# Issue order of wide and narrow matmuls in the projections of a two-layer decoder trunk

## The chip, the cores and the metric

The kernel runs on one core of one Trainium2 chip. The metric is the device time of one execution in microseconds (us); lower is better.

## The reference

The kernel computes two decoder layers on 256 tokens of 2048 channels, all in 32-bit floats. Each layer is a mixer and a feed-forward block, and each of the two ends in a residual sum and a layer norm:

```
x <- LN(alpha * x + mixer(x))      # layer 0: state-space scan + block-sparse attention
                                   # layer 1: three-branch sparse attention + retention
x <- LN(alpha * x + ConvFFN(x))
def conv_ffn(x, w_up, conv_w, conv_b, w_down):
    a, u = jnp.split(x @ w_up, 2, axis=-1)          # 2048 -> 2 x 5632
    a = causal_depthwise_conv(a, conv_w, conv_b)
    return (jax.nn.silu(a) * u) @ w_down            # 5632 -> 2048
```

Nearly all the arithmetic is in the projections: `p = h @ w_in` and `@ w_out` of each mixer, and `w_up` and `w_down` of each feed-forward block.

## The kernel before

**Three products for one.** To keep 32-bit accuracy, every operand of a projection is split into a rounded part ("hi") and the exact rest ("lo"). The activations lie in SBUF as `[128, k, hi|lo]`: for each k-tile of 128 input channels, 512 columns, of which the first 256 are the hi parts of the 256 tokens and the last 256 the lo parts. Weights come from HBM in slabs of up to 512 KB (`wraw`, loaded by the queue of SP, line 102); ScalarE makes `whi` from a slab (line 105) and VectorE makes `wlo` (line 106). The kernel needs hi·hi, hi·lo and lo·hi.

**One unit.** The projections that matter here go through `group_b` (line 200): output channels on partitions, 256 of them in a job, which is a *unit* of two halves `o` of 128 channels. Each half has a PSUM accumulator of 512 columns in a bank of its own. For one k-tile and one half there are two matmuls, each with its own load of a 128x128 weight tile:

- a **wide** one, line 236 (line 240 in the last k-tile): `whi` against all 512 columns of the activation, which gives hi·hi in the left 256 columns of the accumulator and hi·lo in the right ones;
- a **narrow** one, line 237 (line 239 in the last k-tile): `wlo` against the first 256 columns, added to the left 256 columns of the same accumulator.

So a k-tile of a unit is four matmuls. Before, the loop over `o` issues both matmuls of half 0 and then both of half 1: wide, narrow, wide, narrow. In the last k-tile the narrow one comes first in each half: narrow, wide, narrow, wide. After it the evacuation `evac` reads both accumulators. The next job uses the other of two accumulator buffers.

**Jobs.** `x` names the activations of an input or "up" projection (16 k-tiles), `y` those of a mixer's output projection (16 k-tiles), `g` those of a "down" projection (44 k-tiles). `group_b` has, by the tables of jobs in the code, 88 jobs of the two up projections, 14 of the down projections, 14 of the mixers' output projections and 34 of the mixers' input projections: (88 + 14 + 34) x 16 + 14 x 44 = 2,792 k-tiles of four matmuls. The first three jobs of each up projection run as one group, with a third unit in the pool `ps`.

**What else runs on TensorE.** `group_one` (lines 191 to 193) handles the last 256 channels of each output and down projection with narrow matmuls alone; `group_a` (lines 266 to 268) puts tokens on partitions; for the values and gates of retention in layer 1 it has wide matmuls alone. In the mixers' input projections and in the first output jobs, small matmuls of attention and scan (`self.fill`) are handed out between k-tiles, for a single unit after every second one.

TensorE runs its matmuls in the order of the program. Nothing in the kernel sets that order but the order in which the Python code issues them.

Of the kernel before, what the change touches and what calls it, by code (L numbers as in the profile page):

```python
# [13 lines left out]
PSUM = bass.MemoryType.PSUM  # L14
# [11 lines left out]
BIG = 1e30  # L26
# [10 lines left out]


def jobs():
    """The weight groups in the order in which they are used: (source, kind, column parts, k-tiles)."""  # L40
    out = []
    dt, v = EV_DT, EV_V
    out += [("ev_in", "A", cols((dt, 16), (v, 336)), KT), ("ev_in", "A", cols((v + 336, 344)), KT),
            ("ev_in", "A", cols((v + 680, 344)), KT)]
    for c in (EV_B, EV_C, *(EV_XS + 256 * i for i in range(4)), *(EV_Z + 256 * i for i in range(4))):
        out.append(("ev_in", "B", cols((c, 256)), KT))
    for i in range(4):
        out += [("ev_in", "B", cols((EV_Q + 256 * i, 256)), KT), ("ev_in", "B", cols((EV_K + 256 * i, 256)), KT)]
    out += out_jobs("ev_out", KT)
    out += ffn_jobs(0)  # L50
    out += [("od_in", "D", cols((OD_RV, 1024)), KT)]
    out += [("od_in", "A", cols((OD_RG + 512 * i, 512)), KT) for i in range(2)]
    out += [("od_in", "A", cols((OD_VS, 256), (OD_G, 24)), KT), ("od_in", "A", cols((OD_VW, 256)), KT)]
    out += [("od_in", "B", cols((c, 256)), KT) for c in (OD_KC, OD_VC, OD_KS)]
    out += [("cmp0", "C", cols((0, 256)), 16), ("od_in", "B", cols((OD_KW, 256)), KT), ("cmp1", "C", cols((0, 256)), 16)]
    out += [("od_in", "B", cols((OD_Q + 256 * i, 256)), KT) for i in range(4)]
    for i in range(4):
        out += [("od_in", "B", cols((OD_RQ + 256 * i, 256)), KT), ("od_in", "B", cols((OD_RK + 256 * i, 256)), KT)]
    out += out_jobs("od_out", KT)
    out += ffn_jobs(1)  # L60
    return out
# [17 lines left out]


class Weights:
    """Streams the weight slabs: load, then a rounded part and the exact rest for the tensor engine."""

    def __init__(self, tc, pool, streams):
        self.tc, self.nc, self.pool, self.slabs, self.done = tc, tc.nc, pool, [], 0
# [34 lines left out]


class Fill:
    """Work of the mixers that is handed out between weight slabs."""

    def __init__(self):
        self.q = []
        self.rate, self.due = 1.0, 0.0

    def add(self, *steps):
        """Steps; a number stands for so many turns without one."""  # L130
        for x in steps:
            self.q += [lambda: None] * x if isinstance(x, int) else [x]

# [23 lines left out]
class Trunk:  # L157
# [12 lines left out]
        self.nc.scalar.activation(hi, src, AF.Copy)  # L170
        self.nc.vector.tensor_tensor(lo, src, hi.bitcast(F32), op=OP.subtract)  # L171

# [1 line left out]
    def apply_to(self, k):  # L174
        while self.applies and self.applies[0][0] < k:
            self.applies.pop(0)[1]()

    def group_one(self, act, evac):
        """128 output channels, all three products summed in one region."""
        nc, w = self.nc, self.w  # L180
        s = w.first[self.job]
        self.job += 1
        nk = act.shape[1]
        acc = self.acc_pool.tile([128, 2, 512], F32, name="acc")[:, 0, :256]
        k = 0
        while k < nk:
            hi, lo = w.get(s)
            s += 1
            for kk in range(hi.shape[1]):
                xh, xl = act[:, k, :256], act[:, k, 256:]  # L190
                nc.tensor.matmul(acc, hi[:, kk, :], xh, start=(k == 0), stop=False)  # L191
                nc.tensor.matmul(acc, hi[:, kk, :], xl, start=False, stop=False)  # L192
                nc.tensor.matmul(acc, lo[:, kk, :], xh, start=False, stop=(k == nk - 1))  # L193
                k += 1
                if k == nk:
                    evac(acc)
                if k % 2 == 0:
                    self.fill.pop()

    def group_b(self, act, evacs, drain=None):  # L200
        """Output channels on partitions, 256 for each of evacs (or 128); act: [128, k, hi|lo]."""
        nc, w = self.nc, self.w
        first = w.first[self.job]
        self.job += 1
        nk = act.shape[1]
        width = w.slabs[first][4]
        accs = [self.acc_pool.tile([128, 2, 512], F32, name="acc") for _ in evacs[:2]]
        units = [[a[:, o, :] for o in range(min(width // 128, 2))] for a in accs]
        if len(evacs) == 3:
            units.append([self.ps(), self.ps()])  # L210
            accs.append(units[2])
        every = 2 if len(evacs) == 1 else 1
        s = first
        k0 = 0
        held = []
        while k0 < nk:
            m = w.slabs[s][3]
            if s == (None if drain is None else first + drain):
                self.fill.flush()
            self.apply_to(k0 + m + 2)  # L220
            hi, lo = w.get(s)
            s += 1
            if len(units) == 3 and k0 == nk - 2:
                held = [(k0, hi[:, 0], lo[:, 0])]
                k0 += m
                continue
            for kk in range(m):
                part = held + [(k0 + kk, hi[:, kk], lo[:, kk])]
                held = []
                c = 0  # L230
                for unit, evac, whole in zip(units, evacs, accs):
                    for k, h, l in part:
                        for o, acc in enumerate(unit):
                            wh, wl = (a[:, c + 128 * o:c + 128 * o + 128] for a in (h, l))
                            if k < nk - 1:
                                nc.tensor.matmul(acc, wh, act[:, k, :], start=(k == 0), stop=False)  # L236
                                nc.tensor.matmul(acc[:, :256], wl, act[:, k, :256], start=False, stop=False)  # L237
                            else:
                                nc.tensor.matmul(acc[:, :256], wl, act[:, k, :256], start=False, stop=False)  # L239
                                nc.tensor.matmul(acc, wh, act[:, k, :], start=False, stop=True)  # L240
                    if k == nk - 1:
                        evac(whole)
                    c += 128 * len(unit)
                if kk % every == every - 1:
                    self.fill.pop()
            k0 += m

    def group_a(self, act, *evacs):
        """Tokens on partitions; up to 512 output channels for each of evacs."""
        nc, w = self.nc, self.w  # L250
        first = w.first[self.job]
        self.job += 1
# [3 lines left out]
        for s in range(KT // m):  # L256
            self.apply_to(m * s + m + 2)
            hi, lo = w.get(first + s)
            for kk in range(m):
                k = m * s + kk  # L260
                for i, (acc, evac) in enumerate(zip(accs, evacs)):
                    wh, wl = (a[:, kk, i * width:(i + 1) * width] for a in (hi, lo))
                    for t in range(2):
                        xh, xl = act[:, k, t * 128:(t + 1) * 128], act[:, k, 256 + t * 128:256 + (t + 1) * 128]
                        o = acc[:, t, :width]
# [18 lines left out]
            else:  # L284
                nc.vector.scalar_tensor_tensor(d, a[:, :, :256], sign, t, op0=OP.mult, op1=OP.add)

# [1 line left out]
    def out_proj(self, act, pool, idx, room):  # L288
        nc, r, w = self.nc, self.r, self.w
        sacc, qacc = room  # L290
# [119 lines left out]
        if not last:  # L410
            self.w.pump(self.w.limit + 1, pin=True)

# [1 line left out]
    def load_consts(self):  # L414
        nc, I, C = self.nc, self.I, self.consts

# [36 lines left out]
        nc.vector.memset(self.mhalf, -0.5)  # L453

    def bias_scratch(self):
        """Row h: -sqrt(128) * bias of distance j - 127, or BIG where the key is later than the query."""
        nc = self.nc
        self.scr = self.dram.tile([8, 384], F32, name="scr")
        with self.tc.tile_pool(name="bias0", bufs=1) as P:
# [8 lines left out]
            nc.sync.dma_start(self.scr, vv)  # L468

    def load_bias(self, pool, tmp_pool):  # L470
        """nb[q, h, c]: the scratch row at distance 128 + q - c."""
        nc = self.nc
        self.nb = pool.tile([128, H, 256], F32, name="nb")
        s = self.scr[:, :]
# [4 lines left out]
            nc.vector.tensor_copy(self.nb[:, 2 * a:2 * a + 2, :], t[:, :, ::-1])  # L479

    def softmax(self, P, S, nb0, nb1, w0, w1, z, stat, j):
        """exp of scores less their maximum; S: negated raw scores (PSUM), z: out, stat[:, j..j+1]: sums."""
        nc = self.nc
        mn = P.tile([128, 2], F32, name="mn", bufs=4)
        for i, (c, n, nb) in enumerate(((0, w0, nb0), (w0, w1, nb1))):
# [8 lines left out]
            self.fill.add(n, a, b)  # L494

    def attn_steps(self, P, y, ct, h, branches, gate=None, cmp=None):
        """Steps of one head. branches: (qT, kT, v columns of tile t); y[:, ct]: result, hi|lo."""
        nc = self.nc
        st = {}
        nbr = len(branches)  # L500
# [71 lines left out]

        return scores, normalise, mix

# [1 line left out]
    def even(self):  # L576
        nc, x = self.nc, self.x
        with ExitStack() as ctx:
# [209 lines left out]
        steps += [diag(7), 4, rms(1), 1, scale(1)]  # L788
        return steps

# [1 line left out]
    def odd(self):  # L792
        nc, x = self.nc, self.x
        with ExitStack() as ctx:
# [99 lines left out]
                self.out_proj(y, P2, 2, (kv["ks"], kv["kw"]))  # L894

    def compress(self, P, i, xh, xl, kcmp, vcmp):
        """Rows of the 34: 16 blocks of 16 tokens for each kv head, then the position rows; columns: first | second half."""
        nc, w = self.nc, self.w
        first = w.first[self.job]
        self.job += 1  # L900
# [94 lines left out]

        return inner, values, turn

# [1 line left out]
    def ffn(self, layer):  # L999
        nc, x = self.nc, self.x  # L1000
        with ExitStack() as ctx:
# [55 lines left out]
        self.ffn(1)  # L1057


# [1 line left out]
def _pack(w, mine):  # L1061
    parts = []
    for kind, spec, nk in mine:
# [78 lines left out]
```

## Time and profile before

| | |
|---|---|
| time, median of 3 runs | 2367.11 us (2366.61 to 2367.96) |
| span of the profiled execution, first to last instruction | 2365.8 us |
| TensorE busy with matmuls | 2332.8 us, 99% of the span, 13,598 matmuls |
| VectorE busy | 1463.9 us, 62% |
| ScalarE busy | 1166.5 us, 49% |
| mean granted clock of TensorE | 0.992 |
| DMA | 426.28 MB, mean 180 GB/s |

The profile gives the profiled execution's own time as its span; the median of the runs lies 1.3 us above it. A matmul's end is modelled and matmuls overlap in the pipeline, so the length in a matmul's row (0.40 us for a wide one) is longer than its share of the time; what counts here is the distance from one matmul's start to the next one's.

### The profile page before, as it was taken

How to read it: one execution, taken by the hardware profiler on the slowest of the kernel's cores; microseconds unless marked ns; L12 is line 12 of the kernel's file. 1: busy time of each engine (PE TensorE's matmuls, PEld its weight loads, DVE VectorE, ACT ScalarE, POOL GpSimd, SP SyncE). 2: the span in 40 equal slices, each digit the busy share in tenths (PEclk: the TensorE clock that was granted, in tenths of full speed). 3: DMA queues.
4: the chain of work that ended last, by engine and by line, in shares of the span. 5: the costliest groups of instructions: out<-in, count | busy, mean ns of one | idle time of the engine just before them, and what ended most of it. 6: DMA issues, size and time to landing. Idle time of an engine off the chain costs nothing.

```text
span 2365.8 us, 34384 instructions
## 1 busy us (share of the span) xinstructions
PE 2332.8 (99%) x13598; PEld 2044.4 (86%) x13598; DVE 1463.9 (62%) x2095; ACT 1166.5 (49%) x1556; POOL 20.4 (1%) x29
## 2 busy tenths in 40 slices
PE   8999999999999999999999999999999999999997
PEld 8888888888888888889789888888888888888887
DVE  5677567766666664555645667768666666654555
ACT  5555545655555554444545553447555555544443
POOL 0001000000000000000000000000000000000000
PEclk9999999999999999999999999999999999999998
DMA  8664554655555555555557634555555555555553
GB/s 252 189 183 150 162 171 146 199 187 187 187 187 186 188 187 187 187 187 180 184 165 227 191 110 145 169 172 170 187 186 185 187 188 187 187 187 187 189 188 114
DMA packets 124673, 426.28 MB, mean 180 GB/s; under 512 B 13872, under 2 KB 18400, under 8 KB 124384
## 3 DMA queue, kind: packets, MB, share of 16 engines
q1 hardware_dynamic: 124512, 424.09, 56.8%
q8 instruction: 106, 1.74, 0.3%
q14 instruction: 55, 0.45, 0.1%
HBM read 421.93 MB, written 2.11 MB: 179 GB/s over the span
## 4 chain that ended last, share of the span: by engine, by line
PE 88%; issue 10%; DVE 1%; DMA 0%; POOL 0%; ACT 0%; ACTq 0%; SPq 0%; POOLq 0%
PE acc L236 47%; PE acc L237 24%; PE acc L240 3%; PE acc L266 2%; PE acc L267 2%; PE acc L268 2%; PE acc L239 1%; PE acc L191 1%; PE acc L192 1%; PE acc L193 1%; PE ps L570 1%; PE ps L236 1%; DVE r L387 0%; PE ps L237 0%; PE ps L509 0%
## 5 line engine op out<-in xcount | busy, mean ns | idle before, releaser
L106 DVE TENSOR_TENSOR wlo<-wraw,whi 128x1024 fp32r<-128x1024 f32 (+5 forms) x818 | 973.0, 1191 | 669.1 <-ACT whi L105 664.1
L236 PE MATMUL acc<-x,whi 128*128 128x512 f32 x3600 | 1291.2, 401 | 3.4 <-DVE x L403 3.4
L105 ACT ACTIVATE whi<-wraw 128x1024 fp32r<-128x1024 f32 (+5 forms) x818 | 844.3, 1033 | 819.9 <-PE acc L236 587.0
L237 PE MATMUL acc<-x,wlo 128*128 128x256 f32 x3600 | 1012.1, 281 | 0.0
L236 PEld LDWEIGHTS acc<-x,whi 128*128 128x128 f32 x3600 | 677.9, 188 | 163.8 <-DVE x L403 4.0
L237 PEld LDWEIGHTS acc<-x,wlo 128*128 128x128 f32 x3600 | 681.8, 189 | 4.7
L236 PE MATMUL acc<-g,whi 128*128 128x512 f32 x1204 | 422.5, 395 | 0.0
L237 PE MATMUL acc<-g,wlo 128*128 128x256 f32 x1204 | 337.7, 280 | 0.0
L236 PEld LDWEIGHTS acc<-g,whi 128*128 128x128 f32 x1204 | 225.8, 188 | 52.9
L237 PEld LDWEIGHTS acc<-g,wlo 128*128 128x128 f32 x1204 | 227.5, 189 | 0.6
L280 ACT ACTIVATE tmp<-acc 128x512 f32<-128x512 f32 x120 | 71.7, 598 | 207.1 <-PE acc L240 207.1
L236 PE MATMUL acc<-y,whi 128*128 128x512 f32 x420 | 150.4, 400 | 0.0
L237 PE MATMUL acc<-y,wlo 128*128 128x256 f32 x420 | 118.1, 282 | 0.0
L266 PE MATMUL acc<-whi,x 128*128 128x512 f32 (+4 forms) x288 | 101.7, 353 | 7.0 <-ACT whi L105 5.9
L267 PE MATMUL acc<-wlo,x 128*128 128x512 f32 (+4 forms) x288 | 101.2, 352 | 0.3 <-DVE wlo L106 0.3
L268 PE MATMUL acc<-whi,x 128*128 128x512 f32 (+4 forms) x288 | 100.7, 350 | 0.0
L236 PEld LDWEIGHTS acc<-y,whi 128*128 128x128 f32 x420 | 79.0, 188 | 17.8 <-DVE y L171 0.3
L240 PE MATMUL acc<-x,whi 128*128 128x512 f32 x240 | 89.9, 396 | 0.0
L237 PEld LDWEIGHTS acc<-y,wlo 128*128 128x128 f32 x420 | 79.4, 189 | 0.8
L1020 DVE SCALAR_TENSOR_TENSOR c<-fpad,prm,c 128x256 f32<-128x256 f32 x176 | 74.1, 480 | 0.1
L239 PE MATMUL acc<-x,wlo 128*128 128x256 f32 x240 | 68.0, 283 | 0.0
L266 PEld LDWEIGHTS acc<-whi,x 128*128 128x128 f32 x288 | 55.8, 194 | 13.4 <-ACT whi L105 5.9
(304 smaller groups left out, 1754.3 us busy)
## 6 DMA issues: line engine op xcount, KB each, us to landing
wraw<-in_up SPq DMA_DIRECT2D x328, 512.0 KB, 4.1
wraw<-in_down SPq DMA_DIRECT2D x174, 512.0 KB, 4.4
wraw<-in_od_in SPq DMA_DIRECT2D x96, 512.0 KB, 3.7
wraw<-in_ev_in SPq DMA_DIRECT2D x72, 512.0 KB, 3.7
wraw<-in_ev_out SPq DMA_DIRECT2D x32, 512.0 KB, 3.5
wraw<-in_od_out SPq DMA_DIRECT2D x32, 512.0 KB, 3.8
wraw<-in_up SPq DMA_DIRECT2D x32, 384.0 KB, 3.1
wraw<-in_ev_in SPq DMA_DIRECT2D x16, 344.0 KB, 3.5
```

The costliest lines, as they stand in the source:

```text
L105: a = nc.scalar.activation(hi[:, :n], raw[:, :n], AF.Copy)
L106: b = nc.vector.tensor_tensor(lo[:, :n], raw[:, :n], hi[:, :n].bitcast(F32), op=OP.subtract)
L191: nc.tensor.matmul(acc, hi[:, kk, :], xh, start=(k == 0), stop=False)
L236: nc.tensor.matmul(acc, wh, act[:, k, :], start=(k == 0), stop=False)
L237: nc.tensor.matmul(acc[:, :256], wl, act[:, k, :256], start=False, stop=False)
L239: nc.tensor.matmul(acc[:, :256], wl, act[:, k, :256], start=False, stop=False)
L240: nc.tensor.matmul(acc, wh, act[:, k, :], start=False, stop=True)
L266: nc.tensor.matmul(o, xh, wh, start=(k == 0), stop=False)
L267: nc.tensor.matmul(o, xh, wl, start=False, stop=False)
L268: nc.tensor.matmul(o, xl, wh, start=False, stop=(k == KT - 1))
L280: nc.scalar.activation(t, a[:, :, 256:], AF.Copy, scale=sign)
L1020: nc.vector.scalar_tensor_tensor(c[:, i, :], pad[:, i, t:t + 256], w[:, t:t + 1], c[:, i, :], op0=OP.mult, op1=OP.add)
```

## The change

In `group_b`, each k-tile of a unit first issues the wide matmuls of both halves and then the narrow ones of both. In the last k-tile both narrow ones come first and then both wide ones. The operands, the accumulators, the number of matmuls and the number of weight loads are the same; the flags `start` and `stop` mark the same wide matmuls as before. The other lines of the diff take out comments and docstrings, so that line numbers shift by up to two.

```
-                        for o, acc in enumerate(unit):
-                            wh, wl = (a[:, c + 128 * o:c + 128 * o + 128] for a in (h, l))
-                            if k < nk - 1:
-                                nc.tensor.matmul(acc, wh, act[:, k, :], start=(k == 0), stop=False)
-                                nc.tensor.matmul(acc[:, :256], wl, act[:, k, :256], start=False, stop=False)
-                            else:
-                                nc.tensor.matmul(acc[:, :256], wl, act[:, k, :256], start=False, stop=False)
-                                nc.tensor.matmul(acc, wh, act[:, k, :], start=False, stop=True)
+                        wide = [(acc, h[:, c + 128 * o:c + 128 * o + 128], act[:, k, :]) for o, acc in enumerate(unit)]
+                        half = [(acc[:, :256], l[:, c + 128 * o:c + 128 * o + 128], act[:, k, :256])
+                                for o, acc in enumerate(unit)]
+                        for i, (acc, wt, mv) in enumerate(wide + half if k < nk - 1 else half + wide):
+                            nc.tensor.matmul(acc, wt, mv, start=(k == 0 and i < len(unit)),
+                                             stop=(k == nk - 1 and i >= len(unit)))
```

On TensorE, at the end of one job of an up projection and the start of the next, the program before has these rows (line, operation, tiles, partitions x columns); the four rows in the middle are the last k-tile of the job, and the next job begins behind them:

```order
L236 MATMUL acc<-x,whi 128x512
L237 MATMUL acc<-x,wlo 128x256
L239 MATMUL acc<-x,wlo 128x256
L240 MATMUL acc<-x,whi 128x512
L239 MATMUL acc<-x,wlo 128x256
L240 MATMUL acc<-x,whi 128x512
L236 MATMUL acc<-x,whi 128x512
L237 MATMUL acc<-x,wlo 128x256
L236 MATMUL acc<-x,whi 128x512
L237 MATMUL acc<-x,wlo 128x256
```

At the same place of the changed program all these matmuls stand at line 237, and like rows are folded (x2, x4):

```order
L237 MATMUL acc<-x,whi 128x512 x2
L237 MATMUL acc<-x,wlo 128x256 x4
L237 MATMUL acc<-x,whi 128x512 x4
L237 MATMUL acc<-x,wlo 128x256 x2
L237 MATMUL acc<-x,whi 128x512 x2
```

What moved: within a job, wide and narrow now come in twos; at the end of a job four narrow ones stand together, and the two wide ones behind them join the next job's first two.

The second place is inside an input job of layer 0's attention, where the two score matmuls of a head (lines 508 and 509) stand between two k-tiles. Before:

```order
L236 MATMUL acc<-x,whi 128x512
L237 MATMUL acc<-x,wlo 128x256
L236 MATMUL acc<-x,whi 128x512
L237 MATMUL acc<-x,wlo 128x256
L508 MATMUL ps<-k,q 128x128
L509 MATMUL ps<-k,q 128x256
L236 MATMUL acc<-x,whi 128x512
L237 MATMUL acc<-x,wlo 128x256
```

In the changed program these two stand at lines 506 and 507:

```order
L237 MATMUL acc<-x,whi 128x512 x2
L237 MATMUL acc<-x,wlo 128x256 x2
L237 MATMUL acc<-x,whi 128x512 x2
L237 MATMUL acc<-x,wlo 128x256 x2
L506 MATMUL ps<-k,q 128x128
L507 MATMUL ps<-k,q 128x256
L237 MATMUL acc<-x,whi 128x512 x2
```

What moved: only the four matmuls of each k-tile among themselves; the small ones stand between the same k-tiles as before. The order of the DMAs and of GpSimd is unchanged; on ScalarE and VectorE a few instructions change places with a neighbour, in the scan of layer 0 and at the start of each up projection.

## Rows read from the trace of the kernel before

**Rows 1.** The page: the span, and part 1, busy time of each engine.

```profile
span 2365.8 us, 34384 instructions
PE 2332.8 (99%) x13598; PEld 2044.4 (86%) x13598; DVE 1463.9 (62%) x2095; ACT 1166.5 (49%) x1556; POOL 20.4 (1%) x29
```

**Rows 2.** The page, part 4: the chain that ended last, by engine.

```profile
PE 88%; issue 10%; DVE 1%; DMA 0%; POOL 0%; ACT 0%; ACTq 0%; SPq 0%; POOLq 0%
```

**Rows 3.** The page, part 5: wide and narrow matmuls on `x`; last, idle time before them.

```profile
L236 PE MATMUL acc<-x,whi 128*128 128x512 f32 x3600 | 1291.2, 401 | 3.4 <-DVE x L403 3.4
...
L237 PE MATMUL acc<-x,wlo 128*128 128x256 f32 x3600 | 1012.1, 281 | 0.0
```

**Rows 4.** Windows inside an up and a down projection: length, busy PE PEld DVE ACT POOL, clock, DMA.

```profile
480.00:880.00 400.00, 400.00 (x2267) 347.37 (x2266) 245.87 (x285) 207.73 (x249) 0.00 (x0) 1.00 0.58 186
910.00:1090.00 180.00, 180.00 (x1030) 157.37 (x1030) 92.16 (x86) 72.32 (x71) 0.00 (x0) 1.00 0.59 188
```

**Rows 5.** The two longest waits of TensorE: who for whom, us in total, times, longest.

```profile
PE acc L266 <- ACT whi L105: 5.9, 1, 5.9
PE ps L359 <- POOL lnst L368: 5.5, 4, 1.6
```

**Rows 6.** Timeline of TensorE inside an up job: start us, us, engine, line, operation.

```profile
702.16 0.40 PE L236 MATMUL acc<-x,whi 128*128 128x512 f32 x1
...
705.34 0.40 PE L236 MATMUL acc<-x,whi 128*128 128x512 f32 x1
```

**Rows 7.** The same inside a down job.

```profile
935.63 0.39 PE L236 MATMUL acc<-g,whi 128*128 128x512 f32 x1
...
942.56 0.39 PE L236 MATMUL acc<-g,whi 128*128 128x512 f32 x1
```

**Rows 8.** The same in `group_a`, wide matmuls alone.

```profile
1173.44 0.39 PE L266 MATMUL acc<-whi,x 128*128 128x512 f32 x1
...
1177.52 0.39 PE L266 MATMUL acc<-whi,x 128*128 128x512 f32 x1
```

**Rows 9.** The same in `group_one`, narrow matmuls alone.

```profile
1119.98 0.28 PE L191 MATMUL acc<-g,whi 128*128 128x256 f32 x1
...
1123.22 0.28 PE L191 MATMUL acc<-g,whi 128*128 128x256 f32 x1
```

**Rows 10.** Timeline where one up job follows another; PEld is the weight load.

```profile
705.93 0.28 PE L237 MATMUL acc<-x,wlo 128*128 128x256 f32 x1
705.93 0.19 PEld L239 LDWEIGHTS acc<-x,wlo 128*128 128x128 f32 x1
706.05 0.28 PE L239 MATMUL acc<-x,wlo 128*128 128x256 f32 x1
706.05 0.19 PEld L240 LDWEIGHTS acc<-x,whi 128*128 128x128 f32 x1
706.17 0.40 PE L240 MATMUL acc<-x,whi 128*128 128x512 f32 x1
...
706.53 0.39 PE L240 MATMUL acc<-x,whi 128*128 128x512 f32 x1
...
706.76 0.39 PE L236 MATMUL acc<-x,whi 128*128 128x512 f32 x1
...
706.98 0.28 PE L237 MATMUL acc<-x,wlo 128*128 128x256 f32 x1
```

**Rows 11.** Timeline: the first wide matmul of the tenth up job after that.

```profile
819.76 0.39 PE L236 MATMUL acc<-x,whi 128*128 128x512 f32 x1
```

**Rows 12.** Timeline: the first wide matmuls of three down jobs that follow each other.

```profile
918.64 0.39 PE L236 MATMUL acc<-g,whi 128*128 128x512 f32 x1
...
949.16 0.39 PE L236 MATMUL acc<-g,whi 128*128 128x512 f32 x1
...
980.24 0.39 PE L236 MATMUL acc<-g,whi 128*128 128x512 f32 x1
```

**Rows 13.** Timeline: three output jobs, first start, and what follows the third.

```profile
336.19 0.39 PE L236 MATMUL acc<-y,whi 128*128 128x512 f32 x1
...
370.09 0.27 PE L191 MATMUL acc<-y,whi 128*128 128x256 f32 x1
```

## The prediction

> **What bounds the kernel now.** I read the page's busy times first: TensorE has work in flight for 99% of the span, VectorE for 62%, ScalarE for 49% [rows 1]. The chain that ended last is 88% TensorE and 10% "issue", that is, time in which nothing visible was waited for [rows 2]. The groups by line say the same from the other side: before the 3,600 wide matmuls on `x` the engine sat idle for 3.4 us in all, before the narrow ones for none [rows 3]. The windows show that this holds in the stretches that matter: for 400 us of an up projection and 180 us of a down projection TensorE is never without work at full granted clock, VectorE is busy for 61% and 51%, ScalarE for 52% and 40%, the DMA engines for 58% and 59% [rows 4]. TensorE's longest waits are 5.9 and 5.5 us [rows 5]. So the time is the sum of the distances between matmul starts, and nothing else can gain or lose much.
>
> I therefore read those distances. In what follows a **pair** is one wide and one narrow matmul.
>
> - Inside an up job nine pairs take 705.34 - 702.16 = 3.18 us [rows 6], 353.3 ns a pair.
> - Inside one of the down jobs twenty pairs take 942.56 - 935.63 = 6.93 us [rows 7], 346.5 ns a pair.
> - Where all are wide, 18 matmuls take 4.08 us [rows 8], 226.7 ns each. Where all are narrow, 27 take 3.24 us [rows 9], 120.0 ns each. Their sum is 346.7 ns.
>
> So the pair costs what its parts cost alone in the down job, and 6.7 ns more in the up job. The difference of wide and narrow, 226.7 - 120.0 = 106.7 ns for 256 columns, is 2.4 columns a ns, the full clock; each matmul has 13.3 ns on top of its columns. What the change can touch is the extra 6.7 ns alone.
>
> **Where the extra sits.** A job is a fixed row of matmuls, so its length can be counted out. Ten up jobs take 819.76 - 706.76 = 113.00 us [rows 10, 11], 11.300 us each. At 346.7 ns a pair the 32 pairs of a job would be 11.093 us; 0.207 us are extra. Call a narrow matmul right behind a wide one a **switch**. The 15 k-tiles wide, narrow, wide, narrow hold 30 of them, the last one (narrow, wide, narrow, wide) holds 1, and 0.207 us over 31 is 6.7 ns. At the end of the job two narrow ones stand together, 0.12 us apart, and the next narrow-to-wide distance is 0.12 us too; two wide ones stand 0.23 us apart and the next distance is 0.22 us [rows 10]. These are the lone values again, to the 0.01 us of the rows. So the extra goes with switches and not with pairs of the same kind.
>
> The down jobs show that the extra isn't always there. One takes 949.16 - 918.64 = 30.52 us, the next 980.24 - 949.16 = 31.08 us [rows 12], against 88 x 346.7 ns = 30.51 us. The first pays 0.01 us, the second 0.57 us, that is 6.6 ns for each of its 87 switches. The same row of matmuls thus runs in one of two rhythms, which a whole job keeps. These two are the second and the third of a layer's seven down jobs; I take it that the rhythms take turns, which makes four long and three short ones in each layer. The ten up jobs are all long, and I take all 88 to be.
>
> **The change, step by step.**
>
> *What all extras sum to now.* Up: 88 jobs x 0.207 = 18.2 us. Down: eight long jobs x 0.57 and six x 0.01 = 4.6 us. Output projections: three jobs take 370.09 - 336.19 = 33.90 us [rows 13], 11.30 each as above, so 14 x 0.207 = 2.9 us. Input projections: 34 jobs, broken by small matmuls; between 0 (the short rhythm) and 0.207 each (the long one), so 0 to 7.0 us; I take the middle, 3.5, since both rhythms have been seen. Together 29.2 us, 27 to 33 us at the bounds.
>
> *What is left after.* Wide, wide, narrow, narrow has one switch where there were two. A 16-tile job has 15 in place of 31 (the last k-tile, narrow, narrow, wide, wide, has none), a 44-tile job 43 in place of 87. If a switch costs what it does now, job by job, 29.2 x 0.49 = 14.2 us are left and **15 us are saved**. If the six short down jobs fall into the long rhythm, they lose 6 x 43 x 6.7 ns = 1.7 us; with the input projections at their bounds the saving is 12 to 17 us.
>
> *What the new order does to waits.* `wlo` of a slab is first needed one wide matmul later, 0.23 us of slack for VectorE; `whi` is needed by the same first matmul as before. In the last k-tile both narrow ones come first, in the fourth part of a slab that has long been ready. The evacuation still waits for the last wide matmul. TensorE waits for none of these in the trace [rows 3, 5], so I cost them at nothing; the cover is the weight slabs' lead. If TensorE runs 1% faster, VectorE, ScalarE and DMA, all near 60% or below [rows 4], have to run 1% faster too, and can.
>
> *ScalarE and VectorE.* A few neighbours change places at the start of each up projection, where TensorE waits for VectorE's layer norm: the whole of that idle time is 3.4 us [rows 3] and GpSimd's part in the norm 5.5 us [rows 5]. I take nothing, with 1 us either way as the bound, a fraction of those.
>
> *The sum.* The span is 2365.8 us, and the median of the runs 1.3 us above it. 2367.1 - 15 = **2352 us**, with 2349 to 2356 as this case's own range.
>
> [...]
>
> **The rivals.**
>
> 1. *No switch costs anything in the new order (28%).* The extra belongs to a rhythm and not to a switch: the short down job has all 87 switches and pays for none [rows 12]. A new row of matmuls may settle in the short rhythm everywhere, since every second distance is now one between equals, and those cost nothing extra [rows 10]. Against it: the same distances stand at each end of an up job, and the job behind falls back to the long rhythm each time. All 29 us would go: 2338 us.
>
> 2. *Nothing changes (14%).* The extra could be the price of a weight load under a narrow matmul. A load begins when the matmul before it starts (at 705.93 and at 706.05) [rows 10], so the load behind a narrow one has 120 ns, and one behind a wide one 227. The new order shuffles which matmul's load that is, but two in four remain: 32 in a job, as before, and 32 x 6.7 ns = 0.213 us fits the 0.207 nearly as well. Against it: the narrow matmuls in a row [rows 9] load under a narrow one each time and have the same 13.3 ns on top as the wide ones [rows 8]. It gives 2367 us. [...]
>
> 3. *Slower: the price is for a change of accumulator bank (11%).* Before, wide and narrow of a half follow each other in one bank, and the bank changes every second matmul, 32 times in a job. After, it changes with every matmul, 64 times. If that is what costs 6.7 ns, a long job pays 0.427 us in place of 0.213; the extras double, and the time is 2367 + 29 = 2396 us. For it: 32 changes fit an up job to 0.007 us. Against it: ten jobs would show 113.07 us, and the rows say 113.00; and in the wide matmuls in a row the bank changes after every third, at the lone 226.7 ns. It decides from the first k-tile on.
>
> The forecast itself, one price for each switch that is left, has 47%.
>
> **How the numbers follow.** Less than 0.2% (4.7 us) is about what a measurement of this kernel can't tell from no change. The forecast and rival 1 are faster: 75%. Rival 2 is the same: 14%. Rival 3 is slower: 11%. For the range I take the forecast, rival 1 with a microsecond on its far side, and most of rival 2, where part of the saving may show: 2337 to 2366 us leaves out rival 3 and the upper half of rival 2, under 2 in 10.
>
> **What would show it.** In the profile after, an up job should last 11.093 + 15 x 0.0067 = 11.19 us; 11.09 is rival 1, 11.30 rival 2, 11.5 rival 3. Inside a job four matmuls should take 700 ns; their four distances should read about 0.23, 0.23, 0.12, 0.12 with 7 ns more in one of them. TensorE's idle time should stay at a few microseconds, and its clock at 0.99. The prediction is wrong if the two new neighbours bring a rhythm of their own with a third price, which no row here can exclude, since the only doublets seen are at the ends of jobs.

## The result and the profile after

The changed kernel takes **2350.69 us** (median of 4 runs, 2349.53 to 2351.00) against 2367.29 us before: 16.6 us less, a ratio of 0.9927 with a 95% interval of 0.9913 to 0.9941. The forecast was 2352 us.

The page after, its span and part 1, answers to [rows 1]:

```profile
span 2348.5 us, 34385 instructions
PE 2315.6 (99%) x13598; PEld 2036.2 (87%) x13598; DVE 1459.7 (62%) x2095; ACT 1161.3 (49%) x1556; POOL 20.8 (1%) x29
```

The span is 17.3 us shorter and the matmuls' busy time 17.2 us. TensorE's two longest waits after are those of [rows 5], under new line numbers:

```profile
PE acc L264 <- ACT whi L105: 5.9, 1, 5.9
PE ps L357 <- POOL lnst L366: 5.5, 4, 1.6
```

The windows after, in the same two projections as [rows 4] (length, busy PE PEld DVE ACT POOL, clock, DMA), still show TensorE without a gap at full granted clock; in 400 us of the up projection it now starts 2,295 matmuls in place of 2,267:

```profile
480.00:880.00 400.00, 400.00 (x2295) 349.65 (x2294) 247.86 (x287) 207.37 (x251) 0.00 (x0) 1.00 0.56 189
910.00:1080.00 170.00, 170.00 (x977) 148.58 (x976) 88.19 (x84) 68.46 (x67) 0.00 (x0) 1.00 0.56 188
```

So the gain is in the distances. In the changed kernel like matmuls at one line are folded into one row, and where two jobs meet, four wide ones stand in one row (x4). Two of those rows ten up jobs apart, two of down jobs that follow each other, and two k-tiles of a down job with 20 k-tiles from the first start to the last:

```profile
600.77 1.09 PE L237 MATMUL acc<-x,whi 128*128 128x512 f32 x4
...
712.44 1.09 PE L237 MATMUL acc<-x,whi 128*128 128x512 f32 x4
...
910.61 1.09 PE L237 MATMUL acc<-g,whi 128*128 128x512 f32 x4
...
941.28 1.09 PE L237 MATMUL acc<-g,whi 128*128 128x512 f32 x4
...
920.14 0.63 PE L237 MATMUL acc<-g,whi 128*128 128x512 f32 x2
920.61 0.39 PE L237 MATMUL acc<-g,wlo 128*128 128x256 f32 x2
...
934.08 0.63 PE L237 MATMUL acc<-g,whi 128*128 128x512 f32 x2
```

An up job lasts 111.67 / 10 = 11.167 us, where it lasted 11.300 [rows 10, 11]. A down job lasts 30.67 us each time; before, 30.52 and 31.08 took turns [rows 12]. Inside a job four matmuls take 13.94 us / 20 = 697 ns, 3.3 ns over the 693.3 of their parts alone; before it was 706.7 in the long rhythm.

Where the 17.3 us come from, by the job starts in the two traces: the jobs of `group_b` got shorter by 11.0 us in the up projections, 2.3 us in the down projections, 1.1 us in the output projections and 2.2 us in the input projections; 0.6 us lie elsewhere. The short jobs of the down projections got 0.15 us longer each.

### The profile page after: what moved, and what is told of

It is laid out like the page before. It is cut to its first block, busy times and chain, and to the rows that moved or that the text cites. A ratio compares the mean times of both kernels' runs of the same rounds, so it can differ in the third digit from the quotient of the medians.

```text
span 2348.5 us, 34385 instructions
## 1 busy us (share of the span) xinstructions
PE 2315.6 (99%) x13598; PEld 2036.2 (87%) x13598; DVE 1459.7 (62%) x2095; ACT 1161.3 (49%) x1556; POOL 20.8 (1%) x29
## 4 chain that ended last, share of the span: by engine, by line
PE 88%; issue 10%; DVE 1%; POOL 0%; DMA 0%; ACT 0%; ACTq 0%; SPq 0%; POOLq 0%
PE acc L237 74%; PE acc L264 2%; PE acc L265 2%; PE acc L266 2%; PE ps L237 1%; PE acc L191 1%; PE acc L192 1%; PE acc L193 1%; PE ps L568 1%; DVE r L385 0%; PE ps L507 0%; PE ps L534 0%; PE ps L506 0%; PE ps L739 0%; DMA wraw<-in_ev_in 0%
## 5 line engine op out<-in xcount | busy, mean ns | idle before, releaser
L237 PE MATMUL acc<-x,whi 128*128 128x512 f32 x3840 | 1201.5, 398 | 3.4 <-DVE x L401 3.4
L237 PEld LDWEIGHTS acc<-x,wlo 128*128 128x128 f32 x3840 | 706.4, 188 | 159.3 <-issue 0.2
L237 PE MATMUL acc<-x,wlo 128*128 128x256 f32 x3840 | 740.4, 279 | 0.0
L237 PEld LDWEIGHTS acc<-x,whi 128*128 128x128 f32 x3840 | 595.4, 189 | 16.5 <-DVE x L401 4.0
L237 PE MATMUL acc<-g,whi 128*128 128x512 f32 x1232 | 385.1, 395 | 0.0
L237 PE MATMUL acc<-g,wlo 128*128 128x256 f32 x1232 | 240.3, 278 | 0.0
L237 PEld LDWEIGHTS acc<-g,whi 128*128 128x128 f32 x1232 | 188.7, 189 | 1.2
L237 PE MATMUL acc<-y,wlo 128*128 128x256 f32 x448 | 86.5, 279 | 0.0
L281 DVE TENSOR_TENSOR u<-acc,tmp 128x512 f32<-128x512 f32 x44 | 30.4, 692 | 53.6 <-ACT tmp L278 53.6
L281 DVE TENSOR_TENSOR fpad<-acc,tmp 128x512 f32<-128x512 f32 x42 | 29.0, 691 | 51.6 <-ACT tmp L278 51.6
```

The costliest lines, as they stand in the source:

```text
L237: nc.tensor.matmul(acc, wt, mv, start=(k == 0 and i < len(unit)), stop=(k == nk - 1 and i >= len(unit)))
L281: nc.vector.tensor_tensor(d, a[:, :, :256], t, op=OP.add)
```

## The experiments

In all of them the extra of a job is its length less 11.093 us (16 k-tiles) or 30.507 us (44 k-tiles), the time of its parts alone. The code shows the lines that carry each change; the flags `start` and `stop` that follow from it are left out where they add nothing.

**1. Turn every second k-tile round.** Theory: a price for each switch (a narrow matmul right behind a wide one). Rivals: a price for a change of accumulator bank, or for a weight load under a narrow matmul.

```
- ... in enumerate(wide + half if k < nk - 1 else half + wide):
+ ... in enumerate(wide + half if k % 2 == 0 else half + wide):
```

> Every second k-tile is turned round: wide, wide, narrow, narrow, then narrow, narrow, wide, wide. A 16-tile job then has 8 narrow-behind-wide switches in place of 15, a 44-tile job 22 in place of 43; loads and changes of accumulator bank are as many as in the changed kernel. If each switch has a price (3.3 ns as inside the changed kernel's jobs, or 6.7 ns as before): an up job of 11.12 to 11.15 us in place of 11.167, and 2343 to 2347 us in all. If the price is for a change of bank, or for a load under a narrow matmul: as the changed kernel, 2351 us.

It took 2360.74 us, ratio 0.9974 (0.9964 to 0.9984): slower than the changed kernel by 10 us, with half its switches. All three theories miss it. The rows of four wide matmuls, ten up jobs apart:

```profile
600.20 1.09 PE L237 MATMUL acc<-x,whi 128*128 128x512 f32 x4
...
712.47 1.09 PE L237 MATMUL acc<-x,whi 128*128 128x512 f32 x4
```

An up job lasts 11.227 us. The extra is 134 ns for 8 switches, 16.7 ns each, where the changed kernel pays 74 ns for 15.

**2. A whole slab of wide, then a whole slab of narrow matmuls.** `wide` and `half` here hold the eight matmuls of a slab of four k-tiles; the group of three jobs at the start of each up projection keeps the order of the changed kernel.

```
...
+ for group in (wide, half) if k0 + m < nk else (half, wide):
+     for acc, wt, mv, k in group:
+         nc.tensor.matmul(acc, wt, mv, start=(k == 0 and group is wide), stop=(k == nk - 1 and group is wide))
```

> For a whole slab of four k-tiles all eight wide matmuls, then all eight narrow ones (in the last slab narrow first). A 16-tile job has 3 switches, a 44-tile job 10. If each switch has a price of 3.3 to 6.7 ns: an up job of 11.10 to 11.11 us, nearly nothing extra left, and 2341 to 2342 us. If the price is for a change of bank or for a load under a narrow matmul: 2351 us. If long runs of narrow matmuls fall behind on their weight loads (eight loads with 120 ns each): slower than the changed kernel, with narrow matmuls more than 120 ns apart.

It took 2350.71 us, ratio 0.9929 (0.9916 to 0.9941), the same as the changed kernel, with a fifth to a quarter of its switches (3 of 15, 10 of 43). Rows of eight narrow, eight wide and the next narrow ones in a down job:

```profile
926.24 1.11 PE L235 MATMUL acc<-g,wlo 128*128 128x256 f32 x8
927.19 2.00 PE L235 MATMUL acc<-g,whi 128*128 128x512 f32 x8
929.03 0.64 PE L235 MATMUL acc<-g,wlo 128*128 128x256 f32 x4
```

Eight narrow ones take 0.95 us, 0.01 less than alone, and eight wide ones 1.84 us, 0.03 more than alone. The distances of those starts in ns, worked out from the trace:

```
narrow  113 119 120 120 120 120 120 120
wide    234 236 228 232 231 227 227 226
```

The narrow ones don't fall behind. It is the first five wide ones after them that are late, 28 ns in all; 8 of these come back in the first two narrow ones. One switch costs 20 ns here. With the price of a switch at 0 or 6.7 (alternation), 3.3 (twos), 16.7 (fours) and 20 ns (eights), **the theory of a fixed price has fallen**.

**3. The same widths, half the changes of bank**: wide 0, wide 1, narrow 1, narrow 0.

```
+ half = half[::-1]
```

> The changed kernel with the two narrow matmuls of a k-tile in the other order: wide 0, wide 1, narrow 1, narrow 0. The row of widths and the switches are the same, but the accumulator bank changes only 2 times a k-tile in place of 4. If the price is for switches: as the changed kernel, 11.167 us an up job and 2351 us. If it is for changes of bank: half of the 11 us that are still extra go, 2345 us.

It took 2350.82 us, ratio 0.9929 (0.9916 to 0.9943), and ten up jobs last the same 111.67 us:

```profile
600.11 1.09 PE L238 MATMUL acc<-x,whi 128*128 128x512 f32 x4
...
711.78 1.09 PE L238 MATMUL acc<-x,whi 128*128 128x512 f32 x4
```

With half the changes of bank the extra is the same; the third rival is out.

**4. Only the last k-tile changed.**

```
+ row = [p for pair in zip(wide, half) for p in pair] if k < nk - 1 else half + wide
```

> Only the last k-tile of a job is changed (narrow, narrow, wide, wide); all others are wide, narrow, wide, narrow as before. A 16-tile job has 30 switches in place of 31. If each switch has a price of 6.7 ns: 11.293 us an up job and 2366.5 us, no difference that can be measured. If the rhythm that a job falls into at its start sets the price, and the end of the job before sets the rhythm: up jobs may become short, 11.09 us, and the time anywhere down to 2340 us.

It took 2360.23 us, ratio 0.9970 (0.9959 to 0.9980). Three wide matmuls now stand together where two jobs meet; four of those rows:

```profile
592.89 0.87 PE L238 MATMUL acc<-x,whi 128*128 128x512 f32 x3
...
603.99 0.85 PE L238 MATMUL acc<-x,whi 128*128 128x512 f32 x3
...
615.29 0.86 PE L238 MATMUL acc<-x,whi 128*128 128x512 f32 x3
...
626.57 0.87 PE L238 MATMUL acc<-x,whi 128*128 128x512 f32 x3
```

The jobs last 11.10, 11.30 and 11.28 us, and this goes on in threes through both up projections: one job in three is short. All 16 k-tiles hold the same matmuls in the same order in each of them, and still the lengths differ; the buffers take turns in twos and fours, the lengths in threes. So what a job takes must depend on the state in which the row before it left TensorE; call that state its **phase**. My new theory was this: **a row of matmuls has rhythms; which one it takes is a matter of phase, and it keeps it until equal neighbours shift the phase.**

**5. No equal neighbours at all.**

```
+ row = [p for pair in zip(wide, half) for p in pair]     # in the last k-tile too
+ ... stop=(k == nk - 1 and mv.shape[-1] == 256)
```

> Wide, narrow, wide, narrow in every k-tile, the last one too, so that a projection is one unbroken alternation over all its jobs; 32 switches a job. Theory of rhythms (an alternating row runs long, 6.7 ns a switch, or short, 0; it keeps its rhythm until two equal neighbours shift its phase): all jobs of an up projection have one length, all 11.307 us (2368 us in all) or all 11.093 us (about 2345 us), with no turns of short and long as in the run with the last k-tile alone changed. Rival, that something at the start of a job (its evacuation, its first weight slab) sets the rhythm: jobs of both lengths again.

The ten runs took 2345.68, 2346.04, 2346.05, 2348.44, 2358.18, 2359.57, 2360.82, 2372.54, 2373.05 and 2377.37 us: one program, 32 us apart, all at a granted clock of 0.992 or 0.993; the ratio of the medians is 0.996 (0.9929 to 0.9992), and says little. The profiled execution is one of the longer ones (2372.54 us, span 2370.5 us); two wide matmuls 320 pairs apart:

```profile
600.19 0.40 PE L238 MATMUL acc<-x,whi 128*128 128x512 f32 x1
...
713.25 0.40 PE L238 MATMUL acc<-x,whi 128*128 128x512 f32 x1
```

That is 113.06 us, 353.3 ns a pair: all its up jobs are long, and both of its down projections too. No turns of short and long are left, as the theory of rhythms expects. The same execution has the short rhythm as well. Three output jobs of layer 0, and the same three of layer 1:

```profile
326.35 0.40 PE L238 MATMUL acc<-y,whi 128*128 128x512 f32 x1
...
360.27 0.40 PE L238 MATMUL acc<-y,whi 128*128 128x512 f32 x1
...
1541.42 0.40 PE L238 MATMUL acc<-y,whi 128*128 128x512 f32 x1
...
1574.70 0.40 PE L238 MATMUL acc<-y,whi 128*128 128x512 f32 x1
```

They take 33.92 us, 11.307 each, and 33.28 us, 11.093 each, with the same matmuls in the same order. So within one execution the unbroken jobs of a projection keep one rhythm or the other. The scatter of the times would then come from what each projection takes at its start: one up projection of 44 jobs, long or short, is 44 x 0.213 = 9.4 us. That the rhythms differ from one execution to the next is argued from the times; only this execution was profiled.

**6. Narrow matmuls of 192 columns**, in the order of experiment 2; the product of the weights' rest is left out for 64 tokens.

```
- half = [(acc[:, :256], ..., act[:, k0 + kk, :256], k0 + kk)
+ half = [(acc[:, :192], ..., act[:, k0 + kk, :192], k0 + kk)
```

> The slab order with narrow matmuls of 192 columns in place of 256: the product of the weights' rest is left out for the last 64 tokens. If columns set the distance of narrow matmuls: 80.0 + 13.3 = 93 ns apart, 27 ns less for each of 5,584, and 2351 - 149 = 2202 us. If the weight load under them sets it: still 113 to 120 ns apart, and about 2351 us, at least 2310.

It took 2310.52 us (one run). Eight wide, eight narrow, and the next wide ones:

```profile
941.84 2.01 PE L235 MATMUL acc<-g,whi 128*128 128x512 f32 x8
943.69 1.03 PE L235 MATMUL acc<-g,wlo 128*128 128x192 f32 x8
944.56 1.78 PE L235 MATMUL acc<-g,whi 128*128 128x512 f32 x7
```

Eight narrow ones take 0.87 us, the first 0.086 (its load lay under a wide one) and the other seven 112 ns each, not 93; the loads of those behind the second start 111 to 112 ns apart (worked out from the trace). With a load of 128 columns each, narrow matmuls here thus run one every 112 ns at best. The Trainium skill, "TensorE: Matmul & The Clock Gate", section "LDWEIGHTS (loading the stationary operand)", gives 106.7 ns for it (columns over 1.2, an estimate from the page); the run shows 5% more. At 256 columns the narrow ones are 120 ns apart, so there the load is covered, by 8 ns. The changed kernel has as many loads under a narrow matmul as before, and its extra fell; with that the second rival is out.

**7 and 8. Narrow matmuls of 288 columns**, once in the order of experiment 2 and once in that of the kernel before; 32 tokens get a further small product.

```
- acc[:, :256] ... act[:, k, :256]
+ acc[:, :288] ... act[:, k, :288]
```

> The slab order with narrow matmuls of 288 columns: 32 tokens get a further small product. Columns alone would set 133.3 ns. If the wide matmuls behind a narrow run pay for weight loads that have not kept up (the load gets 13 ns more room here): wide matmuls behind it at 227 ns from the first on, an up job of 11.093 + 32 x 0.0133 = 11.52 us. If the first wide ones pay for something else: 234 and 236 ns again, 20 ns extra for each eight and eight, and 11.58 us.

> The order of the kernel before, with narrow matmuls of 288 columns. If the extra of the long rhythm needs narrow matmuls whose columns take just as long as a weight load: a pair at 226.7 + 133.3 = 360.0 ns everywhere and an up job of 11.52 us. If it is a price for any change of width: 366.7 ns a pair and 11.73 us. If it is a matter of phase: anything between, with whole jobs in one rhythm.

They took 2422.45 and 2432.68 us (one run each). Of the first, the wide rows where two jobs meet, nine jobs apart; of the second, two wide matmuls ten pairs apart:

```profile
603.47 3.84 PE L235 MATMUL acc<-x,whi 128*128 128x512 f32 x16
...
707.75 3.84 PE L235 MATMUL acc<-x,whi 128*128 128x512 f32 x16
```

```profile
600.92 0.39 PE L236 MATMUL acc<-x,whi 128*128 128x512 f32 x1
...
604.55 0.39 PE L236 MATMUL acc<-x,whi 128*128 128x512 f32 x1
```

The up job of eights lasts 104.28 / 9 = 11.587 us, 66 ns over 11.52: with 13 ns more room for each load the extra is not smaller than the 60 of experiment 2. The alternating pair takes 363 ns, 3 over 360, a price that no alternation of 256 columns kept for a whole job. So the extra isn't a weight load that has not kept up. It changes with the lengths, as it would with a phase; of what, these two runs don't show.

**9. The other part of the change alone**: twos in all k-tiles but the last, which stays as before.

```
+ row = wide + half if k < nk - 1 else [p for pair in zip(half, wide) for p in pair]
```

> The other part of the change alone: wide, wide, narrow, narrow in all k-tiles but the last, which stays narrow, wide, narrow, wide. If the steady row of twos has one price of 3.3 ns a k-tile, whatever stands at the ends of jobs: as the changed kernel within 1 us, 2351 us, and up jobs within 0.02 us of 11.167 us. If the pair of narrow ones and the pair of wide ones at the end are needed for it: jobs of more than one length, and up to 2367 us.

It took 2350.80 us, ratio 0.9932 (0.9915 to 0.9949). Two up jobs together last 22.34 us, 11.17 each:

```profile
600.14 0.88 PE L238 MATMUL acc<-x,whi 128*128 128x512 f32 x3
...
622.48 0.88 PE L238 MATMUL acc<-x,whi 128*128 128x512 f32 x3
```

The inner k-tiles alone give the whole gain. The last k-tile alone gave 6.6 us (experiment 4), so the gains of the two parts don't add up.

**10. Twelve kinds of job in one run.** If twos bring a job to a fixed phase, a few of them could be used to *choose* the rhythm of an alternation behind them.

```
+ P, flip = 1 + self.job % 12 // 2, self.job % 2
+ alt = [p for pair in (zip(half, wide) if flip else zip(wide, half)) for p in pair]
+ row = wide + half if k < P else alt if k < nk - 1 else half + wide
```

> Each job begins with 1 to 6 k-tiles wide, wide, narrow, narrow and goes on in alternation (wide first in every second job, narrow first in the others); the number goes by the job's place in the list, so that one run shows twelve kinds. If the row of twos brings every job to one phase and the phase at the entry sets the rhythm of the alternation behind it: all jobs of one kind have one length, and some kinds are short (11.10 to 11.13 us, the twos at 3.3 ns each and the rest at 0), others long (11.2 to 11.3). If the rhythm is set by chance: both lengths within one kind.

The one run took 2353.08 us. The extra of an up job in ns, worked out from the job starts in the trace; each kind occurs six to eight times, always behind the same kind, and they agree within 1 ns:

| k-tiles of twos at the start | 1 | 2 | 3 | 4 | 5 | 6 |
|---|---|---|---|---|---|---|
| then wide first | 197 | 10 to 11 | 175 | 25 | 153 | 14 |
| then narrow first | 207 | 7 | 194 | 14 | 28 | 20 |

Four rows where jobs meet, with three whole jobs between them (one k-tile of twos, wide first; one, narrow first; two, wide first):

```profile
600.66 1.08 PE L240 MATMUL acc<-x,whi 128*128 128x512 f32 x4
...
611.94 1.10 PE L240 MATMUL acc<-x,whi 128*128 128x512 f32 x4
...
623.24 1.10 PE L240 MATMUL acc<-x,whi 128*128 128x512 f32 x4
...
634.36 1.08 PE L240 MATMUL acc<-x,whi 128*128 128x512 f32 x4
```

They last 11.28, 11.30 and 11.12 us. In the up projections each kind has one length, short or long, so the length isn't a matter of chance there. But a kind doesn't have its length by itself. In layer 1's output projection a job broken by small matmuls stands before the kind of six k-tiles of twos, narrow first; that one is long there, 156 ns extra in place of 20, and the kind behind it (one k-tile of twos, wide first) is short, 11.10 us in place of 11.28:

```profile
1529.76 1.09 PE L240 MATMUL acc<-y,whi 128*128 128x512 f32 x4
...
1540.86 1.09 PE L240 MATMUL acc<-y,whi 128*128 128x512 f32 x4
```

So the kind and the phase that it meets set the length together.

**11 and 12. The two best kinds for all jobs**: `P, flip = 2, 1` and `2, 0` in the lines above.

> Every job begins with two k-tiles wide, wide, narrow, narrow, goes on with narrow, wide, narrow, wide, and ends with narrow, narrow, wide, wide: the kind that had 0.007 us extra a job in the scan. If the two k-tiles of twos set the phase by themselves: all up jobs at 11.10 us, extras of 1 to 2 us in all, and 2340 us, faster than the changed kernel by 0.4%. If the kind of the job before counts too: long jobs among them, and between 2340 and 2367 us.

> The same with wide, narrow, wide, narrow behind the two k-tiles of twos: the kind that had 0.010 us extra a job in the scan. If the two k-tiles set the phase by themselves: up jobs at 11.10 us and 2340 us. If the job before counts: between 2340 and 2367 us.

They took 2342.76 us, ratio 0.9894 (0.9880 to 0.9909), and 2345.90 us, ratio 0.9908 (0.9892 to 0.9925; its four runs are 2341.08, 2345.05, 2346.76 and 2346.80). Forecast was 2340 for both. The first is clearly faster than both kernels, 7.9 us under the changed one. Its span, and rows where jobs meet, ten up jobs apart:

```profile
span 2340.4 us, 34407 instructions
...
599.22 1.08 PE L240 MATMUL acc<-x,whi 128*128 128x512 f32 x4
...
710.22 1.08 PE L240 MATMUL acc<-x,whi 128*128 128x512 f32 x4
```

An up job lasts 11.100 us: of the 207 ns extra before, 7 are left. In the second kernel's profiled execution ten jobs are as short as their parts alone, 11.093 us each:

```profile
599.05 1.08 PE L240 MATMUL acc<-x,whi 128*128 128x512 f32 x4
...
709.98 1.08 PE L240 MATMUL acc<-x,whi 128*128 128x512 f32 x4
```

That execution is the fastest of its four. The two k-tiles don't set the phase by themselves here either: of layer 1's input jobs the first two that go through `group_b` are long, 11.29 us each; the second of them:

```profile
1252.91 1.09 PE L240 MATMUL acc<-x,whi 128*128 128x512 f32 x4
...
1264.20 1.08 PE L240 MATMUL acc<-x,whi 128*128 128x512 f32 x4
```

In experiment 11 the first of these jobs is long too (11.294 us), but the second is short (11.100). So the phase at the entry counts, as both expectations allowed. In the up projections (from the fourth job on) and in the down projections every job of the two profiled executions is short. Why the times of experiment 12 spread more than those of 11 (2342.28 to 2343.86 us) is not shown; a kind that keeps a long rhythm where it meets one would do it.

## Why the prediction was right

The time lies in the range and 1.3 us from the forecast. What bounds the kernel and the size of the extra held; the step that gives the saving, a fixed price for each switch, did not, and that it came so near is luck.

*What bounds the kernel.* Right: TensorE was busy for 99% before and after, the waits stayed, and the gain is in the distances of matmul starts.

*The extra and its sum.* Right in size: 6.7 ns a pair on average, up jobs at 11.300 us, some 29 us in all, of which the best kernel took out 25. The counts of long jobs were a little too high: in the trace before, the fourth job of each up projection is short (11.10 us), one of the 14 output jobs is short too, and four are broken by small matmuls. The lower bound of the sum is 18.2 + 4.6 + 2.9 = 26 us, not 27; that would put the far end of the case's own range at 2357 us in place of 2356.

*"So the extra goes with switches."* This step failed, though the count of 31 fitted to the nanosecond. With half the switches the extra grew (experiment 1), with a fifth it stayed nearly the same (2), and without equal neighbours one and the same program took 2346 to 2377 us (5). The rows of the kernel before could have shown it. These are the starts of four wide matmuls that follow each other in the long rhythm:

```profile
702.16 0.40 PE L236 MATMUL acc<-x,whi 128*128 128x512 f32 x1
...
702.51 0.40 PE L236 MATMUL acc<-x,whi 128*128 128x512 f32 x1
...
702.87 0.40 PE L236 MATMUL acc<-x,whi 128*128 128x512 f32 x1
...
703.22 0.40 PE L236 MATMUL acc<-x,whi 128*128 128x512 f32 x1
```

The pairs don't pay alike. They take 350, 361 and 349 ns in turn (worked out from the trace), so 3, 14 and 2 ns over 346.7, each with one switch. Only the mean of three is 6.7, and the reading over nine pairs gave that mean. What the runs showed in place of a price is a rhythm of a whole row of matmuls, here one of three pairs.

*"If a switch costs what it does now, 14.2 us are left."* The size was off, for that reason: 29 - 17 = 12 us are left. A k-tile of twos pays 3.3 ns, not 6.7; with 15 x 3.3 = 50 ns and 24 ns more around the end an up job pays 74 ns where I said 100. Worked out by the forecast's own terms, the up projections were to give 9.4 us and gave 11.0, the input projections 1.8 and 2.2, the output projections 1.5 and 1.1, the down projections 2.3 and 2.3. Twos have a rhythm of their own, between the two known ones, and that its 74 ns lie near the 100 of the count is luck: the same reasoning put the kernel of experiment 1 at 2343 to 2347 us, and it took 2360.74.

*The short down jobs.* I left it open whether they lose up to 1.7 us. They lost 0.15 us each, 0.9 us in all.

*The rivals.* The first rival had the right mechanism, rhythm and not switch, and the wrong price for the new row, 0 in place of 3.3; experiments 11 and 12, with other rows, reach its 2338 us to within 5 and 8. The second and the third are out by the result with experiment 6, and by experiment 3. What would make the prediction wrong, a rhythm with a third price, is what happened; it fell between the two that I had bounded it by.

**Still open:** what in the chip sets the rhythm. The runs exclude the number of bank changes, and a load that falls behind under a narrow matmul of 256 columns. They show that wide matmuls behind eight narrow ones are late over five matmuls, and that one and the same row runs in different rhythms behind different rows. Whether two parts of the chip beat against each other, and which, no run here shows. Every matmul here has a weight load of its own; no run has two matmuls on one load, so the loads as one side of the rhythm are not excluded.

## What to carry to other kernels

Where one engine is busy all the time, measure the distance from start to start and compare a row with its parts alone; a remainder of 2% that is the same in every job is worth a few runs. Look at single distances too, and not only at a mean over many. A count that fits one profile to the nanosecond is not yet a cause: change the count, and see whether the price stays. Order can be a free parameter: here two k-tiles in another order at the start of each job took the up and down projections from a bad rhythm into a good one, and a scan of many kinds in one run found them cheaply. A kind that is short in one place can be long behind another row, so it has to be measured in the order in which it will run.

## What was not expected of the hardware

- The same matmuls in the same order run at 353.3 or at 346.7 ns a pair, for whole jobs, by what ran before them (4, 5); without equal neighbours between the jobs one program scatters from 2345.7 to 2377.4 us (5).
- Changing less often between wide and narrow isn't better: 134 ns extra a job in fours, 74 in twos, 60 in eights.
- After eight narrow matmuls of 192 columns, held back by their loads, the first wide one takes 253 ns in place of 227. The load under it starts 22 ns after it, where the loads under the next wide ones start 2 to 4 ns after theirs, and the next matmul starts 231 ns after that load, against 223 to 230 further on (worked out from the starts of experiment 6).
